# A hybrid SSD / chunk-MLP decoder step in float32: where activations are normalised, which engine does the element-wise work, and in which order the tiles of the input projection run

## The chip, the cores and the metric

The kernel runs on one core of a Trainium2 chip. A core has a matrix engine (TensorE, PE in the profile), three engines for element-wise work (VectorE or DVE, ScalarE or ACT, GpSimd or POOL), and a queue (SyncE, SP) that here only issues transfers. The metric is the device time of one execution in microseconds (us). The profile is one execution, recorded instruction by instruction.

## The reference, cut to what matters

288 tokens go through one layer: 256 of a prompt and 8 samples of 4 tokens each. The model dimension is 2048, and everything is float32.

```python
n = rmsnorm(h, g_mix)                       # x * rsqrt(mean(x*x) + eps) * g
proj = n @ w_in                             # 2048 -> 9248 columns, split into z, xbc, dt, u, v
xbc_c = silu(causal_dwconv(xbc, conv0))     # 4 taps along the tokens, 3072 channels
y, ssm_new = ssd(xs, dt, A, Bm, Cm, ssm0)   # four groups of eight heads, chunks of 128 tokens
y_ssd = grouped_rmsnorm((y + d_skip * xs) * silu(z))
u = gelu(u);  v = rmsnorm(gelu(v), g_cm)
y_cm = u * (tril(w_s) @ v + b_s)
h = h + concat([y_ssd, y_cm]) @ w_out
f = rmsnorm(h, g_ffn)
h = h + (silu(f @ w_gate) * (f @ w_up)) @ w_down
h = h + (p @ w_ple) * sigmoid(rmsnorm(h, g_pg) @ w_pg)
return rmsnorm(h, g_final), states
```

## The kernel before

**Layout and products.** Features lie on the 128 partitions and the 288 tokens along the free dimension. A weight tile is [128, 16, 128]: all 2048 inputs of 128 outputs. A float32 product is made of three: weights and activations are each split into two float32r parts, `hi` and `lo`, and `mm3` (L168) adds hi·hi, hi·lo and lo·hi in PSUM. In the trace these are the PE lines L171, L172 and L173, always 128x128 weights times 288 columns. `mtile` (L175) makes one output tile: it loads the weights (`load`, L154, 2048 columns or 1 MB in one transfer on SP's queue, three buffers), splits them 1024 columns at a time (`split_w`, L159: an ACT copy that rounds, L164, then a DVE subtraction, L165; three buffers each), and runs 48 products. 208 such tiles and 32 tiles of the down projection, with 22 input parts each, make nearly all of the PE's work.

**Start.** Fourteen products of ones warm the PE (L221). Then x (L227) and the first weights (L233) come in five parts that grow (`QUANTA`), and each part of x is split with the gain alone (L249). The two first output tiles and the 32 dt columns (L257, four row groups of PSUM at a time) are multiplied part by part. The root mean square of x is found beside it (`x_sumsq`, L261, on POOL and DVE); the projection is linear, so the factor of each token, `rs`, is multiplied into every projected tile later, by a DVE operation on its way out of PSUM (L347, L348, L539, L561).

**Input projection.** 24 tiles of x, B and C come first, each followed by `conv_tile` (L341): DVE applies `rs`, then the four taps run on 256 prompt columns and 32 sample columns apart (L357, L359), with POOL for the edges and the states. When a group's six tiles are there, `ssd_group` (L365) is appended to `side`, a list of Python generators; `advance` (L648) runs the next of them up to its `yield` after each tile, which puts the SSD's small matmuls between the long products. Then come the 16 tiles of the gate z (`z_tile`, L537), two tiles of v, the first half of the output projection (16 tiles), the rest of v, u with the spatial mix, the second half of the output projection, and the FFN.

**POOL's part before.** It forms Rh (L382), x times the decay (L406), the decay of the sample states h0 (L440), the gate product (L543), sums of squares (L134), the spatial mix of the samples (L627, L628) and others, and issues the smaller transfers.

**Order.** The instruction order within an engine comes from a planner in the tile framework, which simulates the program and takes what is ready, earlier lines of the program first. Each engine then runs its instructions in that order and waits on semaphores for the others.

**End.** After the last tile (gate of the input embedding) the final norm's sums (L101), the inverse square root (`rsqrt_compact`, L73, DVE, a chain of small operations), the broadcast (L111, L113) and the scaled output (L841, L843) follow one another.

Of the kernel before, what the change touches and what calls it, by code (L numbers as in the profile page):

```python
# [37 lines left out]
def hybrid_step(ctx: ExitStack, tc: tile.TileContext, xT, wa, wd, wple, pT, vec, cst, wdt, dtal,  # L38
# [51 lines left out]
    def rep4(pool, ap, eng=None):  # L90
        """[128, 32] -> [128, 128]: the sample tokens, four times over."""
        r = pool.tile([P, P], F32, tag="rep4", name="rep4", bufs=2 if pool is cp else 5)
        (eng or nc.gpsimd).tensor_copy(r3(r, 32), bc_mid(ap, 4))
        return r

    def sum_compact(acc):
        """Sums over the partitions of a [128, 288] tile, token-major."""
        ps = big()
        for c in range(3):
            lhs = acc[:, c * P:(c + 1) * P] if c < 2 else rep4(cp, acc[:, 256:288], nc.vector)  # L100
            nc.tensor.matmul(ps[:, c:c + 1], lhsT=lhs, rhs=ones[:, 0:1], start=True, stop=True)  # L101
# [5 lines left out]
    def bcast_tokens(r, keep_psum=False):  # L107
        """[128 tokens, 3] -> a slab with the value of each token on every partition."""
        ps = big()
        for c in range(2):  # L110
# [2 lines left out]
        nc.tensor.matmul(ps[:, 256:288], lhsT=r[0:32, 2:3].to_broadcast([32, P]),  # L113
                         rhs=ident[0:32, 0:32], start=True, stop=True)
# [44 lines left out]
    def split_w(raw, k0, n):  # L159
# [4 lines left out]
        nc.scalar.copy(a, r)  # L164
        nc.vector.tensor_sub(b, r, f32(a))  # L165
# [9 lines left out]
    def mtile(srcs, acts, loaded=None, ps=None):  # L175
        """One output tile: srcs are (dram view [128, k, 128]) in K order."""
        ps = pa.tile([P, NT], F32, tag="acc", name="acc") if ps is None else ps
        total, at = len(acts), 0
        for src in srcs:
            k = src.shape[1]  # L180
            raw = loaded.pop(0) if loaded else load(src, k)
            for k0 in range(0, k, 8) if k > 11 else ((0, 6) if k > 8 else (0,)):
# [758 lines left out]
```

## Time and profile before

| | us |
|---|---|
| median of 3 runs (1781.98 to 1783.4) | 1783.04 |
| span of the profiled execution | 1783.3 |
| busy: PE / weight loads | 1751.2 / 1715.2 |
| busy: DVE / ACT / POOL | 1106.4 / 752.8 / 401.7 |

The profiled execution's span is within 0.3 us of the median. "Busy" counts an engine's instructions from start to end; matmuls overlap, so PE's busy time says that something was in it, not that it ran at its peak. A matmul of two float32 operands appears as two PE records. "PEclk" and "clock" are the share of its full clock that the PE was granted.

### The profile page before, as it was taken

Reading aid. Unit: us, or ns where it says so; the run is one execution under the profiler, and the core shown is the slowest. Engines: PE = TensorE matmul, PEld = TensorE weight load, DVE = VectorE, ACT = ScalarE, POOL = GpSimd, SP = SyncE. Lnnn points to the kernel's source line nnn. Section 1 sums busy time; section 2 is a strip of 40 time slices with the busy share of each in tenths; the row PEclk is TensorE's granted clock in tenths of the full one; section 3 lists DMA queues with packets and bytes.
Section 4 is the critical chain, followed back from the end, with each engine's and each line's share of the span. In section 5 each row is a group of like instructions: output and inputs, shape, how many; then the busy total and the mean of one; then the engine's idle time right before and its main releaser. Section 6 shows DMA issues by size and latency. Waiting matters only on the chain.

```text
span 1783.3 us, 31260 instructions
## 1 busy us (share of the span) xinstructions
PE 1751.2 (98%) x12994; PEld 1715.2 (96%) x12994; DVE 1106.4 (62%) x1598; ACT 752.8 (42%) x1110; POOL 401.7 (23%) x500
## 2 busy tenths in 40 slices
PE   8989999999999999999999999999999999999996
PEld 7968988999999999999999999999999999999996
DVE  7989997865455676665555554444555555555654
ACT  4545544443345444443333333333333333454442
POOL 2665676420024531110000000000000000000133
PEclk9979999999999999999999999999999999999998
DMA  6525554744444444444444444555444444554542
GB/s 244 190 76 197 189 196 156 275 159 166 166 165 166 148 142 166 166 166 163 164 163 165 163 164 137 167 168 188 163 164 164 166 166 151 169 172 154 188 166 77
DMA packets 47084, 297.57 MB, mean 167 GB/s; under 512 B 5360, under 2 KB 6000, under 8 KB 18016
## 3 DMA queue, kind: packets, MB, share of 16 engines
q1 hardware_dynamic: 42544, 271.08, 44.7%
q0 software_dynamic: 3824, 23.34, 3.5%
q8 instruction: 101, 1.65, 0.4%
q10 hardware_dynamic: 576, 1.18, 0.2%
q14 instruction: 39, 0.32, 0.0%
HBM read 283.19 MB, written 12.39 MB: 166 GB/s over the span
## 4 chain that ended last, share of the span: by engine, by line
PE 93%; DVE 3%; issue 2%; POOL 1%; ACT 0%; DMA 0%; SPq 0%; DVEq 0%; POOLq 0%; ACTq 0%
PE acc L171 29%; PE acc L172 29%; PE acc L173 29%; DVE M L396 1%; DVE wlo L165 1%; PE pb L433 1%; PE pb L414 0%; POOL tm L627 0%; DMA xin<-in_xT_dram 0%; PE pb L171 0%; PE pb L173 0%; PE pb L172 0%; POOL sS L628 0%; PE pb L610 0%; PE pb L523 0%
## 5 line engine op out<-in xcount | busy, mean ns | idle before, releaser
L171 PE MATMUL acc<-hi,whi 128*128 128x288 f32 x3984 | 1183.3, 297 | 0.0
L172 PE MATMUL acc<-lo,whi 128*128 128x288 f32 x3984 | 1179.2, 296 | 0.0
L173 PE MATMUL acc<-hi,wlo 128*128 128x288 f32 x3984 | 1174.4, 295 | 0.0
L165 DVE TENSOR_TENSOR wlo<-raw,whi 128x1024 fp32r<-128x1024 f32 (+3 forms) x548 | 661.9, 1208 | 439.7 <-ACT whi L164 437.1
L164 ACT CAST whi<-raw 128x1024 fp32r<-128x1024 f32 (+3 forms) x548 | 539.1, 984 | 805.8 <-PE acc L172 757.4
L171 PEld LDWEIGHTS acc<-hi,whi 128*128 128x128 f32 x3984 | 749.6, 188 | 5.0 <-issue 4.3
L172 PEld LDWEIGHTS acc<-lo,whi 128*128 128x128 f32 x3984 | 750.8, 188 | 2.7 <-issue 1.8
L173 PEld LDWEIGHTS acc<-hi,wlo 128*128 128x128 f32 x3984 | 752.1, 189 | 1.3 <-issue 0.9
L798 POOL TENSOR_TENSOR Up<-Up,G 128x288 f32<-128x288 f32 x44 | 35.6, 810 | 666.9 <-DVE Up L797 652.7
L134 POOL TENSOR_TENSOR sacc<-sacc,sq 128x288 f32<-128x288 f32 x30 | 27.8, 926 | 226.4 <-ACT sq L133 226.4
L792 DVE TENSOR_TENSOR G<-acc,rs 128x288 f32<-128x288 f32 x44 | 20.1, 457 | 43.8 <-PE acc L173 43.8
L797 DVE SCALAR_TENSOR_TENSOR Up<-acc,rs 128x288 f32<-128x288 f32 x44 | 20.1, 457 | 42.6 <-PE acc L173 42.6
L357 DVE SCALAR_TENSOR_TENSOR cva<-cbuf,cwh,cva 128x256 f32<-128x256 f32 x72 | 43.9, 612 | 0.1
L576 POOL TENSOR_SCALAR vS<-ge,vec 128x32 f32<-128x32 f32 x16 | 6.9, 432 | 152.3 <-DVE ge L565 148.3
L440 POOL TENSOR_TENSOR h<-h,decS 128x512 f32<-128x512 f32 x32 | 37.4, 1199 | 0.1
L564 ACT ACTIVATE gt<-gt 128x288 f32<-128x288 f32 x32 | 14.2, 445 | 48.3 <-DVE gt L563 48.3
L144 DVE SCALAR_TENSOR_TENSOR lo<-h,vec,hi 128x288 fp32r<-128x288 f32 x32 | 33.7, 1053 | 0.0
L359 DVE SCALAR_TENSOR_TENSOR cva<-cbuf,cwh,cva 128x32 f32<-128x32 f32 x72 | 29.6, 411 | 2.8 <-POOL cva L355 2.4
L134 POOL TENSOR_TENSOR sacc<-sacc,G 128x288 f32<-128x288 f32 x14 | 18.8, 1341 | 48.8 <-ACT G L133 48.8
L360 ACT ACTIVATE cvt<-cva 128x288 f32<-128x288 f32 x24 | 10.6, 442 | 44.9 <-DVE cva L359 41.3
L642 POOL TENSOR_TENSOR u<-u,s 128x288 f32<-128x288 f32 x16 | 14.9, 939 | 63.9 <-DVE u L565 63.0
L149 ACT CAST hi<-Up 128x288 fp32r<-128x288 f32 x44 | 19.1, 434 | 21.5 <-POOL Up L798 21.5
(288 smaller groups left out, 1169.0 us busy)
## 6 DMA issues: line engine op xcount, KB each, us to landing
raw<-in_wa_dram SPq DMA_DIRECT2D x206, 1024.0 KB, 4.9
raw<-in_wd_dram SPq DMA_DIRECT2D x64, 704.0 KB, 4.1
h<-in_h0T_dram POOLq DMA_DIRECT2D x8, 1024.0 KB, 7.2
out_dram<-h POOLq DMA_DIRECT2D x8, 1024.0 KB, 4.9
h<-in_xT_dram POOLq DMA_DIRECT2D x4, 576.0 KB, 7.7
raw<-in_wple_dram SPq DMA_DIRECT2D x2, 1024.0 KB, 5.1
xin<-in_xT_dram SPq DMA_DIRECT2D x3, 576.0 KB, 8.4
out_dram<-h ACTq DMA_DIRECT2D x4, 288.0 KB, 3.0
```

The source lines that it names most:

```text
L134: nc.gpsimd.tensor_add(self.acc, self.acc, s)
L144: nc.vector.scalar_tensor_tensor(lo, x, gain, f32(hi), op0=ALU.mult, op1=ALU.subtract)
L164: nc.scalar.copy(a, r)
L165: nc.vector.tensor_sub(b, r, f32(a))
L171: nc.tensor.matmul(ps, lhsT=wh, rhs=hi, start=first, stop=False)
L172: nc.tensor.matmul(ps, lhsT=wh, rhs=lo, start=False, stop=False)
L173: nc.tensor.matmul(ps, lhsT=wl, rhs=hi, start=False, stop=last)
L357: nc.vector.scalar_tensor_tensor(a[:, 0:256], pr[:, j:j + 256], wt[j], a[:, 0:256], op0=ALU.mult, op1=ALU.add)
L359: nc.vector.scalar_tensor_tensor(asm, sa[:, :, j:j + 4], wt[j], asm, op0=ALU.mult, op1=ALU.add)
L440: nc.gpsimd.tensor_mul(r3(hh, 64), r3(hh, 64), bc_in(decS[:, 4 * q + i, hs], 64))
L792: nc.vector.tensor_mul(G, pg, rs)
L798: nc.gpsimd.tensor_mul(u, u, G)
```

## The change

The activations are normalised once, before the first product. All of x is loaded in eight parts, on SP's and ACT's queues; ACT squares each part, and 48 one-column matmuls add the squares of all 16 feature tiles in PSUM. From this come the inverse root, its broadcast to all partitions, and eight DVE multiplications of x; only then are the activations split. Three output tiles run side by side from there, and one dt matmul follows each feature tile. No projected tile is multiplied by `rs` any more.

POOL's tensor operations go to DVE and ACT, but for two multiplications at the very end; POOL keeps some memsets and the issue of transfers. The convolution runs on one row of 312 columns, prompt and samples together, and ACT copies the tile out of PSUM. Weights are loaded 1024 columns (512 KB) at a time with four buffers, and their split has a higher priority with the planner. From the second group on, z tiles of the group before are put between the convolution tiles, and gate and norm become generators of their own. The h0 states are handled in four parts instead of two, the v tiles run until the list of generators is empty, and the numbers of some buffers change (rs 1, slab 38, Rh 1, bm 2).

```diff
-    def rep4(pool, ap, eng=None):
-        (eng or nc.gpsimd).tensor_copy(r3(r, 32), bc_mid(ap, 4))
+    def rep4(pool, ap):
+        nc.scalar.copy(r3(r, 32), bc_mid(ap, 4))
+    def sum_tokens(ps, acc, first=True, last=True):
+        for c, t in enumerate((0, P, NT - P)):
+            nc.tensor.matmul(ps[:, c:c + 1], lhsT=acc[:, t:t + P], rhs=ones[:, 0:1], start=first and c == 0,
+                             stop=last and c == 2)
...
-            nc.gpsimd.tensor_add(self.acc, self.acc, s)
+            nc.vector.tensor_add(self.acc, self.acc, s)
...
     def load(src, k):
-        raw = st.tile([P, 2048], F32, tag="raw", name="raw")
+        raw = st.tile([P, 1024], F32, tag="raw", name="raw", bufs=4)
...
+        with tc.high_priority(offset=AHEAD):
+            nc.scalar.copy(a, r)
+            nc.vector.tensor_sub(b, r, f32(a))
...
+    def mtile(src, acts):
+        for k0 in range(0, total, 8):
+            n = min(8, total - k0)
+            w = split_w(load(src[:, k0:k0 + n], n), n)
+            for i in range(n):
+                mm3(ps, w, i, acts[k0 + i], k0 + i == 0, k0 + i == total - 1)
...
+    for q in range(8):
+        (nc.scalar if q % 2 else nc.sync).dma_start(xin[q], xT[:, 2 * q:2 * q + 2])
+    first = {(m, 0): load(wa[m, :, 0:8], 8) for m in range(3)}
+    pss = big("pss")
+    for q in range(8):
+        sq = s0.tile([P, 2, NT], F32, tag="sq", name="sq", bufs=4)
+        nc.scalar.activation(sq, xin[q], AF.Square)
+        for j in range(2):
+            sum_tokens(pss, sq[:, j], first=q + j == 0, last=q + j == 8)
+    halves = {at: split_w(raw, 8) for at, raw in first.items()}
+    rs0 = bcast_tokens(rsqrt_compact(pss[:, 0:3], 2048.0, EPS, "rm"), keep_psum=True)
+    for q in range(8):
+        nc.vector.tensor_mul(xin[q], xin[q], bc_mid(rs0, 2))
+        for k in (2 * q, 2 * q + 1):
+            xk = xin[q][:, k % 2]
+            n_act.append(split(xk, gain=vcol(V_MIX, k), tags=LONG))
+            for m in range(3):
+                if (m, k // 8) not in halves:
+                    halves[m, 1] = split_w(load(wa[m, :, 8:16], 8), 8)
+                mm3(ps01[m], halves[m, k // 8], k % 8, n_act[k], k == 0, k == KD - 1)
+            nc.tensor.matmul(pdt[32 * (k % 4):32 * (k % 4) + 32, 0:NT], lhsT=gw[:, k], rhs=xk,
+                             start=k < 4, stop=k >= 12, tile_position=(0, 32 * (k % 4)))
...
     def conv_tile(i, ps):
+        nc.scalar.copy(cb[:, 3:259], ps[:, 0:256])
+        nc.scalar.copy(new, r3(ps[:, 256:288], 4))
+        nc.scalar.activation(ao, cb[:, 0:NCO], AF.Identity, scale=wt[0], bias=cwh[:, i:i + 1])
         for j in range(1, 4):
+            nc.vector.scalar_tensor_tensor(ao, cb[:, j:j + NCO], wt[j], ao, op0=ALU.mult, op1=ALU.add)
+        nc.scalar.activation(to, ao, AF.Tanh)
...
-            nc.gpsimd.tensor_mul(r3(rh, P), bc_mid(T1, 4), bc_in(f32(dtAh[:, c, k:k + 4]), P))
+            for r, d in ((rh, dtAh), (rl, dtAl)):
+                for i in range(4):
+                    nc.scalar.activation(cols(r, i), T1, AF.Identity, scale=f32(d[:, c, k + i:k + i + 1]))
...
-            nc.gpsimd.tensor_mul(r3(xw, 64), r3(xd, 64), bc_in(dec[:, c, hs], 64))
+            for h in range(8):
+                nc.scalar.activation(xw[:, 64 * h:64 * h + 64], xd[:, 64 * h:64 * h + 64], AF.Identity,
+                                     scale=dec[:, c, 8 * g + h:8 * g + h + 1])
...
         def decay_h0(q):
-                nc.gpsimd.tensor_mul(r3(hh, 64), r3(hh, 64), bc_in(decS[:, 4 * q + i, hs], 64))
+                nc.vector.tensor_mul(r3(hh, 64), r3(hh, 64), bc_in(decS[:, 2 * q + i, hs], 64))
...
+    def z_tile(ps):
+        nc.scalar.activation(t, ps, AF.Tanh, scale=0.5)
+        nc.vector.scalar_tensor_tensor(zr, t, 1.0, ps, op0=ALU.add, op1=ALU.mult)
...
+    for g in range(4):
+        tiles = [16 + g, 20 + g] + list(range(4 * g, 4 * g + 4))
+        for j, i in enumerate(tiles):
+            ps = ps01[at] if at < 3 else mtile(wa[at], n_act)
+            if at == 0:
+                dt_work()
+                decay_work()
+                decay_sample()
+            at += 1
+            conv_tile(i, ps)
             advance(1)
+            if g and j in (1, 2, 4, 5):
+                zs.append(z_tile(mtile(wa[24 + 4 * (g - 1) + len(zs)], n_act)))
+                advance(1)
+        if g:
+            side.append(gate_group(g - 1, zs))
+        side.append(ssd_group(g))
+    for j in range(4):
+        zs.append(z_tile(mtile(wa[36 + j], n_act)))
+        advance(3)
```

More of the change, by code (lines that the diff above doesn't have):

```diff
@@ L173, in mm3 @@
         nc.tensor.matmul(ps, lhsT=wl, rhs=hi, start=False, stop=last)
[L175 to L182, printed above, removed]
-                n = min(8, k - k0) if k > 11 else ((6, k - 6)[k0 > 0] if k > 8 else k)
-                w = split_w(raw, k0, n)
-                for i in range(n):
-                    mm3(ps, w, i, acts[at], at == 0, at == total - 1)
-                    at += 1
+    def mtile(src, acts):
+        ps = pa.tile([P, NT], F32, tag="acc", name="acc")
+        total = len(acts)
+        for k0 in range(0, total, 8):
[3 more added lines that the diff above has]
+                mm3(ps, w, i, acts[k0 + i], k0 + i == 0, k0 + i == total - 1)
         return ps
@@ L211, in hybrid_step @@
     s0 = start.__enter__()
-    xin = [s0.tile([P, 4, NT], F32, name=f"xin{q}") for q in range(4)]
+    xin = [s0.tile([P, 2, NT], F32, name=f"xin{q}") for q in range(8)]
     wdts = s0.tile([P, KD, 32], F32, name="wdts")
@@ L238, in hybrid_step @@
-    w2 = load(wa[2], KD)
-    nc.sync.dma_start(csts, cst)
-    nc.sync.dma_start(dtals, dtal)
-    nc.sync.dma_start(scv, sconv)
-    xk = [xin[k // 4][:, k % 4] for k in range(KD)]
+    nc.scalar.dma_start(csts, cst)
+    first = {(m, 0): load(wa[m, :, 0:8], 8) for m in range(3)}
+    nc.scalar.dma_start(wdts, wdt)
+    nc.scalar.dma_start(dtals, dtal)
+    nc.scalar.dma_start(scv, sconv)
+    pss = big("pss")
[4 more added lines that the diff above has]
+            sum_tokens(pss, sq[:, j], first=q + j == 0, last=q + j == 8)
@@ L349, in conv_tile @@
-        nc.gpsimd.tensor_copy(cvo[:, i, 0], pr[:, 256:259])
-        nc.gpsimd.tensor_copy(cvo[:, i, 1:9], sa[:, :, 4:7])
-        a, t = slab(name="cva"), slab(name="cvt", tag="ta")
-        asm = r3(a[:, 256:288], 4)
+        sd = sd_box["pool"]
+        cb, a, t = (sd.tile([P, NCV], F32, tag=n, name=n, bufs=b) for n, b in (("cbuf", 3), ("cva", 2), ("cvt", 2)))
+        nc.gpsimd.memset(cb[:, 0:3], 0.0)
+        nc.scalar.copy(cb[:, 259:NCV].rearrange("p (b t) -> p b t", t=7)[:, :, 0:3], scv[:, i])
@@ L449, in ssd_group @@
         R0 = [make_R(0, hb) for hb in range(2)]
-        xrep = [rep4(sd, xs[j][:, 256:288]) for j in range(4)]
         yield
@@ L474, in ssd_group @@
         yield
+        xrep = [rep4(sd, xs[j][:, 256:288]) for j in range(4)]
         M1 = [seg(r) for r in R1]
@@ L512, in ssd_group @@
         nc.scalar.copy(xst, xwr)
-        for q in (32, 96):
-            nc.gpsimd.tensor_sub(xst[q:q + 32], xwr[q:q + 32], f32(xst[q:q + 32]))
-        decay_h0(0)
+        nc.vector.tensor_sub(xst[64:128], xwr[64:128], f32(xst[64:128]))
+        for q in range(4):
+            decay_h0(q)
         yield
@@ L684, in hybrid_step, with mlp_pools @@
-    nc.gpsimd.dma_start(o_conv, cvo)
-    pend = None
-    for g in range(4):
+    hp_box, mid_box = {}, []
+    def mlp_pools():
+        sd_pool.__exit__(None, None, None)
+        hp = ctx.enter_context(tc.tile_pool(name="hp", bufs=1))
+        h = hp.tile([P, KD, NT], F32, name="h")
+        mlp = tc.tile_pool(name="mlp", bufs=1)
+        mp = mlp.__enter__()
+        for q in range(4):
+            nc.gpsimd.dma_start(h[:, 4 * q:4 * q + 4], xT[:, 4 * q:4 * q + 4])
+        return hp, h, mlp, mp, spatial_weights(mp)
@@ L719, in hybrid_step @@
+    side.append(gate_group(3, zs))
+    nvt = 0
+    while side or nvt < 2:
+        v_tile(nvt, mtile(wa[56 + nvt], n_act), nv)
+        nvt += 1
+        advance(1)
+        if 3 in ssd_done and not hp_box and not any(x.__name__ == "ssd_group" for x in side):
+            hp_box["pools"] = mlp_pools()
+    hp, h, mlp_pool, mp, sw = hp_box["pools"]
     for m in range(KD):
-        ps = mtile([wa[40 + m]], ycat[:16])
+        ps = mtile(wa[40 + m], ycat[:16])
         nc.vector.tensor_add(h[:, m], h[:, m], ps)
-    for i in range(2, KD):
-        ps = mtile([wa[56 + i]], n_act)
+    for i in range(nvt, KD):
+        ps = mtile(wa[56 + i], n_act)
```

263 lines of the change are left out of this document (86 added, 177 removed).

## The prediction

> **What bounds the kernel now.** The page comes first: span, busy times, clock line, chain by engine.
>
> ```profile
> span 1783.3 us, 31260 instructions
> PE 1751.2 (98%) x12994; PEld 1715.2 (96%) x12994; DVE 1106.4 (62%) x1598; ACT 752.8 (42%) x1110; POOL 401.7 (23%) x500
> PEclk9979999999999999999999999999999999999998
> PE 93%; DVE 3%; issue 2%; POOL 1%; ACT 0%; DMA 0%; SPq 0%; DVEq 0%; POOLq 0%; ACTq 0%
> ```
>
> PE holds 93% of the chain. Faster element-wise work is worth something only where PE waits or runs at a lower clock. The view of stretches says where that is (stretch, length, busy of PE with records, of PEld, DVE, ACT, POOL, granted clock, DMA):
>
> ```profile
> 0.00:40.00 40.00, 31.41 (x205) 27.55 (x206) 31.90 (x41) 17.59 (x30) 13.01 (x14) 0.91 0.69 246
> 80.00:112.00 32.00, 32.00 (x205) 27.35 (x207) 29.02 (x56) 19.61 (x48) 22.59 (x33) 0.89 0.31 107
> 112.00:140.00 28.00, 20.96 (x139) 17.87 (x132) 22.37 (x26) 4.70 (x6) 14.48 (x19) 0.76 0.12 39
> 140.00:200.00 60.00, 59.15 (x408) 50.84 (x408) 58.67 (x104) 29.50 (x61) 41.05 (x64) 0.97 0.55 198
> 200.00:300.00 100.00, 100.00 (x725) 86.86 (x723) 87.38 (x144) 49.97 (x101) 70.64 (x84) 1.00 0.52 188
> 300.00:350.00 50.00, 49.46 (x358) 48.15 (x358) 42.36 (x74) 21.96 (x36) 23.95 (x25) 0.97 0.72 265
> 600.00:650.00 50.00, 49.12 (x381) 48.72 (x380) 36.77 (x64) 21.71 (x34) 26.98 (x40) 1.00 0.42 136
> 650.00:1764.00 1114.00, 1114.00 (x8377) 1113.68 (x8377) 609.14 (x759) 456.70 (x613) 107.82 (x118) 1.00 0.48 162
> ...
> 87.20:94.10 6.90, 6.90 (x29) 6.34 (x30) 6.35 (x13) 3.19 (x11) 4.73 (x8) 0.52 0.44 153
> 118.00:131.60 13.60, 8.74 (x40) 7.57 (x41) 11.16 (x12) 1.49 (x2) 7.80 (x10) 0.51 0.08 11
> ```
>
> From 650 to 1764 us PE never stops: 1114.00 / 8377 = 0.133 us a record. Nothing that the change does to the FFN can show there. A stretch's loss is its idle time plus half of the busy time that it spent at half clock (clock 0.89 over 32 us means 7 us at half):
> - 112 to 140: 7.0 idle, and half of the 8.7 busy us of 118 to 131.6, together 11.4 us
> - 80 to 112: 3.5; 140 to 200: 0.85 + 1.8 = 2.7; 300 to 350: 0.5 + 1.5 = 2.0; 600 to 650: 0.9
> - 0 to 40: 8.6 idle, of which 1.5 lies before the first product, and 3.4 for the clock, so 10.5 after it.
>
> About 31 us in all, 20 of them after the start. That, and the time to the first product, is what can change.
>
> **The part that it removes.** The timeline explains 112 to 140:
>
> ```profile
> 100.89 0.68 DVE L396 TENSOR_TENSOR M<-M,cbm 128x512 f32<-128x512 f32 x1
> ...
> 112.85 9.95 DVE L396 TENSOR_TENSOR M<-M,cbm 128x512 f32<-128x512 f32 x1
> ...
> 113.54 8.03 POOL L440 TENSOR_TENSOR h<-h,decS 128x512 f32<-128x512 f32 x8
> ```
>
> The same DVE mask takes 0.68 us and, where eight POOL decays run back to back, 9.95. PE waits for it and then runs at half clock. With these products off POOL, the 11.4 us go. The spatial mix leaves POOL too (0.9). Of the other 8.2 us (3.5 + 2.7 + 2.0) most is clock, after spells of narrow matmuls (below), which stay in the program; I count 2 as gained by the z tiles between them, between 0 and 8.2. The stage takes on work for which I put 2 us of new stalls (0 to 20, third rival). Stage: -11.4 - 0.9 - 2 + 2 = -12.3 us.
>
> **The part that it adds: the start.** Products now wait for all of x, 48 one-column sums, a root and a broadcast. The old start:
>
> ```profile
> 0.99 5.32 PE L221 MATMUL warm<-ones 128*128 128x128 f32 x28 [0.99 <-POOL cbuf L345]
> 6.78 0.40 PE L171 MATMUL ps<-hi,whi 128*128 128x288 f32 x1 [0.46 <-ACT whi L164]
> ...
> L101 PE MATMUL pb<-ones,sacc 128*128 128x1 f32 x32 | 4.0, 229 | 0.0
> L257 PE MATMUL pdt<-xin,gw 128*32 128x288 f32 x32 | 3.5, 466 | 0.0
> L488 PE MATMUL pb<-S,cva 128*128 128x512 f32 x8 | 4.4, 632 | 0.0
> ```
>
> The first product runs at 6.8. In the new start the warm-up ends at 6.3 as before; x (2.4 MB) needs about 9 to 10 us at the 246 GB/s of the first 40 us, so the sums, not the loads, decide. L101 has two records a matmul (32 for 16), so 48 sums are 96 records. Their rate hangs on the clock:
>
> ```profile
> 1.20:5.20 4.00, 4.00 (x20) 4.00 (x21) 1.00 0.82 206
> 5.40:6.40 1.00, 0.91 (x9) 0.72 (x7) 1.00 0.87 293
> ...
> 85.80:87.20 1.40, 1.40 (x14) 0.93 0.00 0
> 87.20:88.00 0.80, 0.80 (x4) 0.50 0.00 0
> ...
> 0.00:10.00 10.00, 8.48 (x49) 7.21 (x49) 3.95 (x6) 4.43 (x8) 2.50 (x8) 1.00 0.81 258
> 10.00:20.00 10.00, 4.89 (x31) 3.29 (x31) 10.00 (x5) 8.35 (x15) 9.73 (x6) 0.83 1.04 403
> ```
>
> The first two rows are the warm-up alone (L221): 0.2 us a record until 5.2, then 0.11, so the clock doubles at about 5.3 (the clock column shows no lower clock there, but the spacing does). The next two are L332, matmuls of 32 columns: 0.1 us a record, then 0.2; the clock falls at 87.2 although PE had work all the time. Narrow matmuls do not hold the clock. The two low stretches shown above last 6.9 and 13.6 us, two and four times 3.4, so I take 3.4 us as the grain: the next decision after 5.3 falls at 8.7, in a stretch with 1 us of warm-up and otherwise one-column sums, and I expect half clock from there. Then 21 records at 0.112 us from 6.3 to 8.7 and 75 at 0.213 (the slow warm-up's spacing, nearer than any other row), 16.0 us: the last sum is at 24.7. At full clock all along it would be 6.3 + 96 x 0.112 = 17.1.
>
> On this point the Trainium skill ("TensorE: Matmul & The Clock Gate", Part 1) says that a monitor of how busy the PE is sets the clock, and that sustained activity of some 3.4 us releases it. Read plainly, a steady run of sums would keep the clock, and the sum would be that of the first rival; the L332 row, where it fell in the middle of such a run, is against it.
>
> From the sums to the first product, the tail of the old kernel has the same steps:
>
> ```profile
> 1768.99 0.36 PE L101 MATMUL pb<-ones,rep 128*128 128x1 f32 x2
> 1773.59 0.40 ACT L837 COPY rsb<-pb 128x288 f32<-128x288 f32 x1 [5.12 <-PE pb L113]
> ...
> L843 DVE TENSOR_TENSOR h<-h,pb 128x576 f32<-128x576 f32 x6 | 4.1, 748 | 2.3 <-ACT rsb L837 2.3
> ...
> L143 ACT ACTIVATE hi<-xin,vec 128x288 fp32r<-128x288 f32 x16 | 7.4, 525 | 5.1 <-DMA xin<-in_xT_dram 5.1
> ```
>
> 1769.3 (end of the sums) to 1773.6 is 4.2 us with the broadcast at half clock, 3.4 at full. One scaling of two feature tiles takes 0.75, one rounding 0.53. First product: 24.7 + 4.2 + 0.75 + 0.53 = 30.2 us (full clock: 21.7).
> The splits that feed PE then:
>
> ```profile
> L144 DVE SCALAR_TENSOR_TENSOR lo<-cva,vec,hi 128x288 fp32r<-128x288 f32 x16 | 8.2, 544 | 0.2 <-ACT hi L143 0.2
> ...
> L164 ACT CAST whi<-raw 128x1024 fp32r<-128x1024 f32 x418 | 437.8, 1048 | 637.8 <-PE acc L172 592.1 <-issue 30.3 <-PE ps L172 3.2
> ...
> 103.56 1.21 DVE L165 TENSOR_TENSOR wlo<-raw,whi 128x1024 fp32r<-128x1024 f32 x1
> ```
>
> For two feature tiles DVE needs 0.75 + 2 x 0.54 = 1.8 us, PE 18 products, 2.4, so PE sets the pace.
>
> Further terms:
> - The dt matmuls lose their neighbours in the other row groups. Before, 32 records took 3.5 us. Alone, a record scales from L488 (4.4 / 8 = 0.55 at 512 columns, 0.31 at 288, with overlap about 0.24): 7.7 to 9.9 us in place of 3.5. I take the lower, +4.3.
> - The old sums and the old broadcast of the root, 12 records of 0.12, leave this place: -1.5.
> - The old stalls of the start go: -10.5.
> - New stalls: three buffers each of whi and wlo hold the first halves of three tiles until their last product, so the second halves are split while PE waits: a copy of 1.05 and three subtractions of 1.2 against about 2 us of other work, 1.5 to 3; I take 1.5. And about 2 at half clock until it rises again (1 to 3.4).
>
> Start: (30.2 - 6.8) + 4.3 - 1.5 - 10.5 + 3.5 = +19.2 us. Written for the time T of the first product, start and stage together give 1783.3 + T - 23.3.
>
> **What I cost at nothing.**
>
> ```profile
> SPq L156 <- DVE wlo L165: 1510.3, 258, 24.5
> ```
>
> The missing `rs` product, DVE's sums of squares and gate products in the FFN: from 650 on DVE is busy for 609 of 1114 us, and PE waits for none of it; some 0.45 us more for each 12.8 us changes no product's start. Loads of 512 KB: SP's queue waits for free buffers (1510 us for L165, the row above), not for data, and four buffers hold 2 MB, or 12.8 us of products; uncovered, a late load would cost its lateness at each of some 440 places, which I find unlikely at a DMA share of 0.48. The tail keeps its chain; the column scaling that moves from POOL to ACT lies beside the sums.
>
> **The rivals.**
> - *The clock stays full during the sums.* T = 21.7 and 1.5 us of new stalls for 3.5: 1783.3 + 21.7 - 23.3 - 2.0 = 1779.7. For it: the clock stayed full in the first 10 us and fell to 0.83 only in the next ten, with few products. Against it: L332. It is the way that the Trainium skill's rule, above, would have it.
> - *The sums hide behind the loads* (faster). If weight loads for one-column products run well under 0.11 us, the sums end with x at about 11 us: T = 11 + 3.4 + 1.3 = 15.7, 1783.3 + 15.7 - 23.3 - 2.0 = 1773.7. It decides at T = 23.3, or 25.3 with those smaller stalls; from 21.7 down the kernel is faster by 0.2% or more. Against it: 4.0 us for 32 records of L101.
> - *ACT becomes the bound of the SSD stage.*
>
> ```profile
> L384 ACT ACTIVATE Rl<-cst,dtAl 128x128 fp32r<-128x128 f32 x64 | 20.4, 390 | 4.6 <-PE pb L390 4.6
> ...
> L466 ACT COPY btm<-pb 128x256 f32<-128x256 f32 x4 | 1.4, 360 | 2.5 <-PE pb L464 2.5
> ```
>
>   From 200 to 300 ACT is busy for 50 us and DVE for 87. A group gains on ACT 16 pieces of Rh, 24 of x times decay, the copies out of PSUM and the states of six tiles, at up to 0.36 to 0.39 us each in the rows above and about 0.2 for the smallest, some 20 us, and the z tiles' share of splits. I estimate 65 to 70 of 83 us (ten tiles of 6.4 and the SSD's own matmuls) for both engines, close enough that short pieces ahead of a weight copy could stop PE at each tile: 40 tiles x 0.3 = 12 us more, 1802.
> - *The planner orders it otherwise*, so that little of this happens: around 1783.
>
> **How the numbers follow.** Forecast 1783.3 + 19.2 - 12.3 = 1790.2, so 1790; span and median differ by 0.3 us, so no correction. Its own range is 1784 to 1797 (the dt term, the clock after the start, 0 to 8.2 of narrow spells). Chances: forecast 0.50, full clock 0.22, ACT 0.17, hidden sums 0.06, planner 0.05. 0.2% (3.6 us) is about what a measurement of this kernel can tell from no change. Faster: half of the full clock, the hidden sums, a part of the planner, 0.19. Same: the other half, the forecast's lower end, 0.22. Slower: 0.59. The range leaves out the hidden sums, the low end of full clock, and half of the ACT case: 1775 to 1803.
>
> **What would show it.** PE's L-line of the sums with 96 records and its spacing (0.11 or 0.21); the first product near 30; no DVE mask over 1 us; no stall between 112 and 140 but a low clock after the narrow spells; ACT's busy share of the SSD stage near 80%; 0.133 us a record in the FFN as before. A first product before 20, or a spacing in the FFN other than 0.133, would make the prediction wrong.

## The result and the profile after

The changed kernel takes 1803.66 us (median of 4 runs, 1801.47 to 1804.6) against 1783.22 for the kernel before: the ratio is 1.0102, with a 95% interval of 1.0084 to 1.012. (It is not the quotient of these two medians, 1.0115, which the interval holds too.) The changed kernel is 1.0% slower. The profiled execution of the changed kernel took 1801.47 us, its span is 1799.3; in all profiled runs below the device time is about 2 us above the span. Spans are compared with spans.

The page of the changed kernel, span, busy times and granted clock in 40 slices:

```profile
span 1799.3 us, 31672 instructions
...
PE 1765.1 (98%) x13084; PEld 1731.5 (96%) x13084; DVE 1062.1 (59%) x1655; ACT 826.9 (46%) x1432; POOL 31.2 (2%) x79
...
PEclk6999999999999999999999999999999999999998
```

POOL does next to nothing now (401.7 us before), ACT has gained 74 us, and PE is still busy for 98% of the span. Two slices of the clock have changed visibly: the first has fallen from 0.9 to 0.6, and the third has risen from 0.7 to 0.9. The view of stretches, whose columns are those of the prediction, has the rest:

```profile
10.90:31.50 20.60, 20.59 (x96) 20.55 (x96) 4.59 (x5) 7.53 (x12) 0.00 (x0) 0.50 0.54 189
...
80.00:112.00 32.00, 32.00 (x239) 31.53 (x239) 21.29 (x37) 24.42 (x69) 0.40 (x4) 1.00 0.44 147
112.00:140.00 28.00, 28.00 (x201) 21.95 (x200) 21.17 (x37) 19.73 (x57) 0.65 (x2) 1.00 0.35 123
140.00:200.00 60.00, 60.00 (x452) 59.17 (x452) 46.28 (x91) 35.06 (x84) 4.78 (x13) 1.00 0.63 213
200.00:300.00 100.00, 100.00 (x733) 91.80 (x732) 76.55 (x145) 73.38 (x198) 5.51 (x16) 1.00 0.52 170
300.00:350.00 50.00, 50.00 (x371) 44.20 (x371) 41.84 (x77) 27.53 (x70) 4.81 (x9) 1.00 0.61 193
350.00:420.00 70.00, 65.54 (x465) 58.03 (x464) 50.25 (x103) 42.28 (x106) 7.08 (x14) 0.95 0.47 157
420.00:445.00 25.00, 18.97 (x121) 17.93 (x121) 13.30 (x23) 7.50 (x11) 0.34 (x1) 0.86 0.72 264
...
900.00:1300.00 400.00, 400.00 (x3010) 400.00 (x3009) 204.20 (x247) 147.41 (x169) 0.00 (x0) 1.00 0.52 165
```

Three things are to be seen. From 80 to 350 PE is busy all the time at clock 1.00, where before it stood 7 us between 112 and 140 and ran at 0.76 to 0.97 in four of the stretches: by the prediction's rule (idle time plus half of the time at half clock) all of the 3.5 + 11.4 + 2.7 + 2.0 us are gone. In the first row 96 records take 20.6 us at clock 0.50: the sums. And two stretches in which the kernel before had no loss have one now: 350 to 420 (4.5 idle, clock 0.95) and 420 to 445 (6.0 idle, clock 0.86), together 10.5 us idle and up to 7 us for the clock, some 15 to 17. The last row is the FFN: 400 / 3010 = 0.133 us a record, as before. The kernel before in the two stretches:

```profile
350.00:420.00 70.00, 70.00 (x528) 69.68 (x527) 49.92 (x91) 34.60 (x52) 17.91 (x16) 1.00 0.47 163
420.00:445.00 25.00, 25.00 (x192) 25.00 (x191) 11.29 (x13) 8.42 (x8) 0.00 (x0) 1.00 0.50 169
```

**The start.** The timeline of the changed kernel (start, length, engine, line; in brackets the idle time before it and what ended it):

```profile
5.04 0.34 ACTq L229 DMA_DIRECT2D cst<-in_cst_dram  x1
6.64 0.34 ACTq L231 DMA_DIRECT2D wdts<-in_wdt_dram  x1
8.34 0.34 ACTq L232 DMA_DIRECT2D dtal<-in_dtal_dram  x1
9.79 0.33 ACTq L233 DMA_DIRECT2D scv<-in_sconv_dram  x1
10.17 2.40 ACT L239 ACTIVATE sq<-xin 128x576 f32<-128x576 f32 x4 [7.49 <-DMA cst<-in_cst_dram]
...
10.91 2.29 PE L102 MATMUL pss<-ones,sq 128*128 128x1 f32 x10 [3.69 <-ACT sq L239]
...
35.50 5.41 DVE L249 TENSOR_TENSOR xin<-xin,pb 128x576 f32<-128x576 f32 x8 [1.58 <-PE pb L120]
...
36.88 0.85 PE L179 MATMUL ps<-hi,whi 128*128 128x288 f32 x2 [1.42 <-ACT hi L150]
...
37.90 3.78 PE L257 MATMUL pdt<-xin,gw 128*32 128x288 f32 x32
```

The first product is at 36.9 us, not 6.8. ACT issues four small loads ahead of its first square, and they leave its queue only 1.5 to 1.7 us apart, though each takes 0.34. So the first square comes at 10.2, PE stands idle from the end of the warm-up to 10.9, and the 96 sums run at half clock from the first to the last. (The bracket of the square names the load of cst. That load landed 6.2 us after its issue, at 11.2, which is after the square had begun, so it is not what the square waited for.) Behind the sums and the root, DVE scales all eight parts of x, 5.41 us, before it computes its first lo. The dt products, in one block, fill PE's time until the first product with a lo runs at 41.6.

**The stall at 366 to 372.** The timeline there:

```profile
366.73 1.27 ACT L366 ACTIVATE Rl<-cst,dtAl 128x128 fp32r<-128x128 f32 x4
...
367.90 2.01 ACT L389 ACTIVATE xw<-xdt,dec 128x64 f32<-128x64 f32 x8
368.06 0.50 PE L372 MATMUL pb<-Rl,Ur 128*128 128x512 f32 x1 [1.60 <-ACT Rl L366]
369.81 0.53 ACT L150 ACTIVATE hi<-cvo,vec 128x288 fp32r<-128x288 f32 x1
...
370.37 0.52 DVE L151 SCALAR_TENSOR_TENSOR lo<-cvo,vec,hi 128x288 fp32r<-128x288 f32 x1 [2.43 <-ACT hi L150]
370.90 0.82 DVE L526 SCALAR_TENSOR_TENSOR zr<-zt,acc 128x288 f32<-128x288 f32 x2
...
371.41 0.61 PE L179 MATMUL acc<-hi,whi 128*128 128x288 f32 x1 [2.86 <-DVE zr L526]
```

Read from below: PE waits 2.86 us for an accumulator that zr, the DVE product that empties a z tile, has not emptied; zr stands on DVE behind a lo; lo waits 2.43 for its hi; and hi stands on ACT behind eight 64-column pieces of the weighted x (xw). The four pieces before those, Rl (the lo part that goes with Rh), made PE wait 1.60.

**The stall at 430 to 435**, in the timeline, and behind it three lines of the DMA view of 410 to 440 (transfers: number, KB each, us from issue to landing):

```profile
432.09 2.29 DVE L576 TENSOR_TENSOR wsr<-wsr,cst 128x2048 f32<-128x2048 f32 x1 [5.00 <-DMA wsr<-in_wsT_dram]
434.30 1.18 DVE L707 TENSOR_TENSOR h<-h,acc 128x288 f32<-128x288 f32 x3
...
434.89 0.58 PE L179 MATMUL acc<-hi,whi 128*128 128x288 f32 x1 [4.41 <-DVE h L707]
```

```profile
raw<-in_wa_dram SPq DMA_DIRECT2D x7, 512.0 KB, 5.9
h<-in_xT_dram POOLq DMA_DIRECT2D x4, 576.0 KB, 7.1
wsr<-in_wsT_dram POOLq DMA_DIRECT2D x1, 1024.0 KB, 12.6
```

The mask of the spatial weights (L576), on POOL before, is on DVE now. It waits 5.00 us there for a load that takes 12.6 us beside four parts of h and seven weight loads, and holds up three residual additions (L707) that would have emptied accumulators: PE waits 4.41.

### The profile page after: what moved, and what is told of

Same layout as the page of the kernel before. It is cut to its first block, busy times and chain, and to the rows that moved or that the text cites. A ratio compares the mean times of both kernels' runs of the same rounds, so it can differ in the third digit from the quotient of the medians.

```text
span 1799.3 us, 31672 instructions
## 1 busy us (share of the span) xinstructions
PE 1765.1 (98%) x13084; PEld 1731.5 (96%) x13084; DVE 1062.1 (59%) x1655; ACT 826.9 (46%) x1432; POOL 31.2 (2%) x79
## 4 chain that ended last, share of the span: by engine, by line
PE 75%; DVE 0%; ACT 0%; DVEq 0%; issue 0%
PE acc L179 25%; PE acc L181 24%; PE acc L180 24%; PE pb L597 0%; PE pb L181 0%; PE pb L179 0%; PE pb L180 0%; PE pb L589 0%; DVE h L829 0%; PE pb L102 0%; PE pb L118 0%; DVE wlo L173 0%; DVE h L707 0%; PE pb L120 0%; DVEq L916 0%
## 5 line engine op out<-in xcount | busy, mean ns | idle before, releaser
L172 ACT CAST whi<-raw 128x1024 fp32r<-128x1024 f32 (+1 forms) x516 | 533.7, 1035 | 827.8 <-PE acc L180 664.8
L173 DVE TENSOR_TENSOR wlo<-raw,whi 128x1024 fp32r<-128x1024 f32 (+1 forms) x516 | 623.3, 1208 | 486.2 <-ACT whi L172 479.5
L778 DVE TENSOR_TENSOR G<-acc,rs 128x288 f32<-128x288 f32 x44 | 20.1, 457 | 41.6 <-PE acc L181 41.6
L338 DVE SCALAR_TENSOR_TENSOR cva<-cbuf,cwh,cva 128x312 f32<-128x312 f32 x72 | 38.5, 538 | 1.3 <-ACT cva L336 0.4
L389 ACT ACTIVATE xw<-xdt,dec 128x64 f32<-128x64 f32 x96 | 24.4, 338 | 5.9 <-DVE xdt L386 5.9
L102 PEld LDWEIGHTS pss<-ones,sq 128*128 128x128 f32 x96 | 20.6, 333 | 3.9 <-ACT sq L239 3.9
L102 PE MATMUL pss<-ones,sq 128*128 128x1 f32 x96 | 20.6, 352 | 3.7 <-ACT sq L239 3.7
L418 DVE TENSOR_TENSOR h<-h,pb 128x512 f32<-128x512 f32 x32 | 20.9, 680 | 1.1 <-PE pb L417 1.1
L366 ACT ACTIVATE Rh<-cst,dtAh 128x128 fp32r<-128x128 f32 x64 | 20.6, 397 | 1.5 <-PE pb L371 1.5
L784 DVE TENSOR_TENSOR Up<-Up,G 128x288 f32<-128x288 f32 x44 | 20.2, 458 | 1.5
L366 ACT ACTIVATE Rl<-cst,dtAl 128x128 fp32r<-128x128 f32 x64 | 20.8, 399 | 0.0
```

The costliest lines, as they stand in the source:

```text
L102: nc.tensor.matmul(ps[:, c:c + 1], lhsT=acc[:, t:t + P], rhs=ones[:, 0:1], start=first and c == 0, stop=last and c == 2)
L338: nc.vector.scalar_tensor_tensor(ao, cb[:, j:j + NCO], wt[j], ao, op0=ALU.mult, op1=ALU.add)
L366: nc.scalar.activation(cols(r, i), T1, AF.Identity, scale=f32(d[:, c, k + i:k + i + 1]))
L389: nc.scalar.activation(xw[:, 64 * h:64 * h + 64], xd[:, 64 * h:64 * h + 64], AF.Identity, scale=dec[:, c, 8 * g + h:8 * g + h + 1])
L418: nc.vector.tensor_add(h0[q][:, i], h0[q][:, i], ps)
L784: nc.vector.tensor_mul(u, u, G)
```

## The experiments

The theory: the change gains about 20 us in the SSD stage by taking work off POOL; it loses 30 at the start; and it adds two waits in queues that had room before. The main rival for each part was that the loss has another cause and only moves. Eleven kernels were run. "T" is the first product, "rest" the span less T: what a start costs shows in T, what a later stall costs in the rest. Each ratio is against the kernel before as it ran beside that experiment (medians of 1782.49 to 1784.55). Span, T and rest are of one profiled execution each; the spans of one kernel differ by 1 to 5 us between its executions, so a difference of less than 2 or 3 us in the rest counts only where the medians agree.

| kernel | median us | ratio (95%) | span | T | rest |
|---|---|---|---|---|---|
| before | 1783.22 | | 1783.3 | 6.78 | 1776.5 |
| changed | 1803.66 | 1.0102 (1.0084, 1.012) | 1799.3 | 36.88 | 1762.4 |
| e1 mask on POOL | 1797.64 | 1.0083 (1.0068, 1.0098) | 1796.8 | 36.59 | 1760.2 |
| e2 wide sums | 1794.85 | 1.0065 (1.005, 1.008) | 1794.3 | 29.75 | 1764.6 |
| e3 small loads off ACT | 1794.96 | 1.0066 (1.0051, 1.0081) | 1793.3 | 30.00 | 1763.3 |
| e4 before, decay on DVE | 1769.07 | 0.9929 (0.9911, 0.9948) | 1766.3 | 6.31 | 1760.0 |
| e5 mask moved | 1801.53 | 1.0103 (1.0084, 1.0122) | 1801.6 | 36.94 | 1764.7 |
| e6 z first | 1802.9 | 1.011 (1.0091, 1.0128) | 1801.4 | 36.95 | 1764.5 |
| e7 before, start free of POOL | 1763.19 | 0.9888 (0.9867, 0.9908) | 1760.0 | 6.78 | 1753.2 |
| e8 all parts | 1790.07 | 1.0038 (1.0024, 1.0052) | 1788.6 | 24.55 | 1764.1 |
| e9 mask after the root | 1796.23 | 1.0069 (1.005, 1.0088) | 1793.0 | 36.71 | 1756.3 |
| e10 weighted x on DVE | 1794.09 | 1.0056 (1.004, 1.0072) | 1795.1 | 36.69 | 1758.4 |
| e11 four mends | 1779.38 | 0.9968 (0.9958, 0.9979) | 1776.6 | 24.06 | 1752.5 |

### The start: e2 and e3

e2 makes the sums 128 columns wide instead of one:

```diff
-            sum_tokens(pss, sq[:, j], first=q + j == 0, last=q + j == 8)
+            for c, t in enumerate((0, P, NT - P)):
+                nc.tensor.matmul(pss[:, c * P:(c + 1) * P], lhsT=sq[:, j, t:t + P], rhs=ones,
+                                 start=q + j + c == 0, stop=q + j == 8 and c == 2)
```

> The changed kernel with the 48 sums of the start 128 columns wide instead of one (the ones matrix whole as moving operand, the root read from one column of each block); the same number of records and weight loads. My theory: the 0.213 us a record of the sums is the half clock, and it is half because one-column products do not count as work for the clock. Expected: the clock stays or becomes full during the sums, 0.112 us a record, the sums take 11 to 14 us instead of 20.6, first product 7 to 10 us earlier, span 1789 to 1793. Rival: the sums are bound by loading 128x128 float32 weights at the start, whatever the clock counts; then wide sums take as long or longer (0.213 or more a record) and the span does not fall.

The view of stretches of e2, cut where the granted clock changes:

```profile
9.60:16.40 6.80, 5.44 (x26) 5.44 (x27) 1.68 (x3) 4.21 (x7) 0.00 (x0) 0.51 1.02 380
16.40:26.70 10.30, 8.03 (x72) 7.84 (x71) 4.76 (x15) 3.94 (x6) 0.00 (x0) 0.99 0.57 180
```

The same 96 records begin at the same time, at 0.21 us each (5.44 / 26), but the clock then rises and the others take 0.112 (8.03 / 72). T falls by 7.1 us. With one column the clock stayed at 0.50 for 20.6 us although PE was busy for 20.59 of them. The Trainium skill ("TensorE: Matmul & The Clock Gate", Part 1) has the clock released by some 3.4 us of sustained activity. These two runs show that the one-column matmuls did not count as such activity and the 128-column ones did.

e3 issues the small loads from POOL:

```diff
-    nc.scalar.dma_start(csts, cst)
+    nc.gpsimd.dma_start(csts, cst)
...
-    nc.scalar.dma_start(scv, sconv)
+    nc.gpsimd.dma_start(scv, sconv)
```

> The changed kernel with four small loads of the start (constants, dt weights, dt vectors, convolution states) issued by POOL instead of ACT. My theory: ACT stands in these issues until 10.1 us because its queue takes no more than the four parts of x at once, so the first square starts at 10.2 although x's first part landed some 4 us earlier. Expected: first square at 5 to 6 us, first sum right after the warm-up at 7 to 7.5, sums end 3 to 4 us earlier, and since little idle time is left between warm-up and sums the clock may stay full for one more stretch of 3.4 us: span 3 to 6 us shorter, 1793 to 1796. Rival: the squares wait for x to land, not for the issues; then nothing moves by more than 1 us.

The timeline of e3:

```profile
6.26 18.42 PE L102 MATMUL pss<-ones,sq 128*128 128x1 f32 x96
...
30.00 0.85 PE L179 MATMUL ps<-hi,whi 128*128 128x288 f32 x2 [1.41 <-ACT hi L150]
```

The sums begin at 6.26, right behind the warm-up, and end at 24.7. The four loads alone cost 6.9 us. What holds ACT's queue is not shown directly: in the changed kernel SP's queue, too, issued nothing between its four parts of x and 5.2 us, and there the view of waits names the loads of x as what it waited for. In all of after, e2, e3 and e8 the rest of the kernel is the same within 2.2 us (1762.4 to 1764.6): each microsecond of T is a microsecond of the time.

### The stage before: e4 and e7

e4 is the kernel before with one word changed, the decay of h0 on DVE:

```diff
-                nc.gpsimd.tensor_mul(r3(hh, 64), r3(hh, 64), bc_in(decS[:, 4 * q + i, hs], 64))
+                nc.vector.tensor_mul(r3(hh, 64), r3(hh, 64), bc_in(decS[:, 4 * q + i, hs], 64))
```

> The kernel before with one part of the change alone: the decay of the sample states (32 products of 128x512) on DVE instead of POOL. My theory: the stall of the kernel before at 112 to 140 us is one DVE mask held up for 9.9 us beside eight of these products on POOL. Expected: no DVE mask over 1.5 us, no stall there, span 8 to 12 us shorter than 1783.3, 1771 to 1775, although DVE gets 22 us more work. Rival: DVE is already busy for 80 to 97% in this stage, so 22 us more on it delay the weight splits, and the span stays or grows (1783 to 1795).

The view of stretches of e4:

```profile
80.00:112.00 32.00, 32.00 (x216) 26.01 (x214) 29.74 (x56) 20.02 (x49) 23.08 (x34) 0.95 0.32 108
112.00:140.00 28.00, 27.65 (x207) 25.52 (x204) 28.00 (x54) 12.79 (x26) 17.68 (x21) 1.00 0.39 127
140.00:200.00 60.00, 59.40 (x435) 52.54 (x434) 59.74 (x117) 31.49 (x64) 30.59 (x58) 1.00 0.62 212
```

PE's records from 112 to 140 go from 139 to 207 at clock 1.00, and the kernel is 0.7% faster. Its span is 17.0 us shorter, more than the 8 to 12 expected, since the losses after 140 have shrunk as well: in the third row above, 2.7 us have become 0.6 of idle time, and from 300 to 350 2.0 have become 0.2 (0.24 idle, clock 1.00). In e4 no z tiles stand between the convolution tiles. So most of what the kernel before lost there went with the decays, and z tiles were not needed for it. The loss before 112 cannot be the decays', whose first runs at 113.5; it is 3.5 us in the kernel before, 1.6 in e4 and 0.4 in e7 below, with the same sixteen 32-column matmuls (L332) in each, and what decides it stays open.

The Trainium skill ("SBUF — State Buffer", Who interferes with whom) says that a DVE instruction with two inputs in SBUF and a GpSimd instruction that reads SBUF exclude each other. The runs agree that one waits for the other. The DVE mask of 9.95 us shows more than that: DVE can be kept out over all of eight POOL instructions in a row, not over one.

The largest loss left in e4 is of the same kind (timeline of e4):

```profile
10.29 2.59 POOL L264 TENSOR_TENSOR sq<-xin 128x1152 f32<-128x1152 f32 x1 [0.72 <-DMA xin<-in_xT_dram]
...
10.84 9.73 DVE L144 SCALAR_TENSOR_TENSOR lo<-xin,vec,hi 128x288 fp32r<-128x288 f32 x4
...
12.96 2.74 POOL L266 TENSOR_TENSOR sq<-sq,sq 128x1152 f32<-128x1152 f32 x1
...
15.66 4.60 POOL L264 TENSOR_TENSOR sq<-xin 128x1152 f32<-128x1152 f32 x2
...
21.77 0.61 PE L173 MATMUL ps<-hi,wlo 128*128 128x288 f32 x1 [7.23 <-DVE wlo L165]
```

Four lo that take 1.80 us elsewhere take 9.73 beside POOL's squares and the addition between them, which run without a pause worth naming from 10.3 to 20.3. e7 takes them off POOL too:

```diff
-            nc.gpsimd.tensor_mul(sq[q], xin[q], xin[q])
+            nc.scalar.activation(sq[q], xin[q], AF.Square)
...
-                nc.gpsimd.tensor_add(sq[0], sq[0], sq[1])
+                nc.vector.tensor_add(sq[0], sq[0], sq[1])
```

> The kernel before with the decay on DVE, as in e4, and also the start's squares on ACT and their first add on DVE, so that POOL has no tensor work while the first products run. Theory (the largest loss left in e4, 7.5 us at 14 us, was a lo of DVE held up beside POOL's squares): it goes, and 1769 becomes 1757 to 1764. Rival (ACT's squares of 0.9 to 1.1 us each stand between the early copies and the first products wait for those instead): 1766 to 1772, no gain over e4.

1763.19 us: within the theory, and the fastest kernel of all, 1.1% below the one before, with three lines changed. The stretch from 0 to 42 of e7, where PE was busy for 33.41 us at clock 0.92 in the kernel before:

```profile
0.00:42.00 42.00, 37.81 (x270) 34.07 (x271) 29.39 (x59) 25.00 (x39) 3.64 (x14) 1.00 0.76 268
```

### The mask of the spatial weights: e1, e5, e9

e1 puts L576 back on POOL:

```diff
-        nc.vector.tensor_mul(w, w, bc_mid(T1, KD))
+        nc.gpsimd.tensor_mul(w, w, bc_mid(T1, KD))
```

> The changed kernel with one instruction put back: the mask of the spatial weights (128x2048) runs on POOL, not DVE. My theory: in the changed kernel DVE stands for 5.0 us before this mask, which waits for its weights from HBM, and 2.3 us in it, with three residual additions and three weight splits queued behind; PE idles for 6.5 us between 420 and 437 us and then has half clock for 6.8. Expected: DVE takes the additions before 432, PE does not stop there, span 8 to 9 us shorter than the changed kernel's 1799.3, about 1791. Rival: the additions wait for h itself, which is loaded just before (10 us to landing); then the stall stays, only the 2.3 us of the mask go, and the span is 1797.

It gained less than the theory asked for. The profiled execution has a span of 1796.8, the rival's number, but it is the longest of its four, and that of the changed kernel is the shortest of its four; the medians are 6.0 us apart. The rival's reason is not what happened: the additions begin at 431.1 and have waited for PE, not for h. A line of the timeline of e1, the instructions of the tile wlo in e1, between 432 and 443 (minimum, median and maximum in ns), and PE's stretch:

```profile
431.14 1.18 DVE L707 TENSOR_TENSOR h<-h,acc 128x288 f32<-128x288 f32 x3 [2.90 <-PE acc L181]
```

```profile
L173 DVE TENSOR_TENSOR wlo<-raw,whi x4: 1212/1214/5618, 432.2 to 440.0; 128x1024 fp32r<-128x1024 f32 x4
```

```profile
420.00:445.00 25.00, 20.70 (x149) 19.53 (x148) 17.89 (x29) 8.21 (x11) 7.13 (x5) 1.00 0.80 293
```

The wait for the load went to POOL, where nothing waits behind it; but then the mask runs 5.48 us on POOL, from 432.4, and one weight subtraction on DVE takes 5.6 us instead of 1.2. It is the kind of collision that e4 removed, at another place. PE still idles for 4.3 us, but its clock stays at 1.00.

e5 moves the product in the program, to the first line of `spatial`, and keeps it on DVE:

```diff
-        nc.vector.tensor_mul(w, w, bc_mid(T1, KD))
         return bss, wss, w, b
...
     def spatial(nv, mp, bss, wss, w, b):
+        nc.vector.tensor_mul(w, w, bc_mid(T1, KD))
```

> The changed kernel with one DVE instruction moved: the product of the spatial weights with the mask is issued at the start of the spatial step and no longer where the weights' loads are issued; it stays on DVE. Theory (DVE stood 5 us before this product, for a load that had not landed, with the residual adds and a lo of the product stream queued behind it, and PE lost 8 to 9 us at 420 to 440 with the half clock that followed): the stall there goes, 1801.5 becomes about 1793, and DVE has no wait of over 1 us for a DMA at that line. Rival (the loads saturate the DMA share there and PE waits for weights anyway): within 3 us of the changed kernel, the wait only moves to another line.

Nothing happened: the timeline of e5 has the product, from its new line, in the same place and with the same wait.

```profile
434.02 2.29 DVE L579 TENSOR_TENSOR wsr<-wsr,cst 128x2048 f32<-128x2048 f32 x1 [4.78 <-DMA wsr<-in_wsT_dram]
436.23 1.18 DVE L707 TENSOR_TENSOR h<-h,acc 128x288 f32<-128x288 f32 x3
```

The planner makes the order, and it takes what is ready by its own simulation, in which the load is presumably there by then (not shown). So e5 says nothing about the cause. e9 gives the product a third factor, a one computed from the root of v, so that it has to come later:

```diff
-        nc.vector.tensor_mul(w, w, bc_mid(T1, KD))
...
+        one = mp.tile([P, 1], F32, name="one")
+        nc.vector.tensor_scalar(one, r[:, 0:1], 0.0, 1.0, op0=ALU.mult, op1=ALU.add)
+        nc.vector.scalar_tensor_tensor(w, w, one[:, 0:1], bc_mid(T1, KD), op0=ALU.mult, op1=ALU.mult)
```

> e5 changed nothing, since the order of DVE's work is made by the planner and it put the moved product back in front of the residual adds. Here the same product on DVE has a third factor, a one worked out from the root of v, so that it can only come after the v tiles. Theory (DVE's 5 us wait for a load in front of the residual adds is the cause of the stall at 420 to 437 us): with it gone PE loses less than 2 us there, and 1801.5 becomes 1792 to 1795. Rival (the residual itself, or the weights, land as late, since the DMA share is 1.0 there): the wait moves to the residual adds or a weight copy and the time stays within 3 us.

```profile
420.00:445.00 25.00, 22.51 (x164) 21.58 (x164) 14.07 (x21) 10.30 (x13) 0.00 (x0) 1.00 0.82 291
```

This stretch of e9 has 164 records where the changed kernel has 121, and the clock stays at 1.00. The rest falls by 6.1 us (1762.4 to 1756.3), the median by 7.4, to just above the 1792 to 1795 expected. The theory holds, with 2.5 us of idle time still there, short waits for split weights.

### The z tiles: e6 and e10

e6 puts the Tanh and zr of a z tile at the planner's high priority:

```diff
-        nc.scalar.activation(t, ps, AF.Tanh, scale=0.5)
-        nc.vector.scalar_tensor_tensor(zr, t, 1.0, ps, op0=ALU.add, op1=ALU.mult)
+        with tc.high_priority(offset=AHEAD):
+            nc.scalar.activation(t, ps, AF.Tanh, scale=0.5)
+            nc.vector.scalar_tensor_tensor(zr, t, 1.0, ps, op0=ALU.add, op1=ALU.mult)
```

> The changed kernel with the two operations that empty a z tile's accumulator (ACT's Tanh and DVE's product) at the high priority that the product stream's splits have. Theory (PE waited 3 us at 368 us for an accumulator that zr had not yet emptied, since zr stood on DVE behind a lo that waited for ACT's small pieces, and half clock followed, 7 us in all): PE's wait there falls below 1 us and 1801.5 becomes 1795 to 1798. Rival (ACT is simply full there and the order of its queue is what counts): zr comes no earlier, since its Tanh stands behind the same pieces, and the time stays within 2 us.

DVE took some zr earlier than before, but the time did not change, as the rival had it. The waits of e6 between 360 and 380 (us in total, times, longest) are those of the changed kernel:

```profile
PE acc L179 <- DVE zr L527: 2.9, 1, 2.9
...
DVE lo L151 <- ACT hi L150: 2.6, 2, 2.4
```

e10 instead shortens what stands ahead on ACT:

```diff
-            for h in range(8):
-                nc.scalar.activation(xw[:, 64 * h:64 * h + 64], xd[:, 64 * h:64 * h + 64], AF.Identity,
-                                     scale=dec[:, c, 8 * g + h:8 * g + h + 1])
+            nc.vector.tensor_mul(r3(xw, 64), r3(xd, 64), bc_in(dec[:, c, hs], 64))
```

> The changed kernel with the weighted x of the SSD stage as one DVE product of 128x512 in place of eight ACT pieces of 128x64. Theory (the stall at 366 to 376 us comes from ACT's queue: Rl and hi stand behind eight pieces of 2.0 us in all, lo waits for hi, and zr and the accumulator for lo): PE's waits there shrink from 4.5 us to below 1, the half clock behind them goes, and 1801.5 becomes 1794 to 1796. Rival (the group is full anyway: DVE gains 24 x 0.7 = 17 us in all, its lo come later and PE waits for those): 1799 to 1806.

Waits and the stretch from 360 to 380 in e10:

```profile
PE acc L179 <- DVE zr L524: 0.9, 1, 0.9
```

```profile
360.00:380.00 20.00, 19.13 (x132) 15.66 (x131) 17.13 (x30) 13.67 (x34) 0.55 (x1) 1.00 0.41 132
```

The wait is 0.9 us, the clock 1.00, the rest 4.0 us shorter; the median is 9.6 lower, and the profiled execution, at 1796.88 us, is the longest of its four. The cause of this stall is ACT's row of small pieces.

### Together: e8 and e11

e8 joins e2, e3, e5 and e6 and writes all dt products behind the product stream's, with the first splits at high priority.

> The changed kernel with the parts together: sums 128 columns wide, the small loads issued by POOL, the mask product later, the z tiles' two operations first, and at the start all dt products behind the product stream's, with the splits of the first tiles at high priority. Theory (each part was its own loss): the gains of the wide sums (6.6) and of the small loads (6.5) overlap in part, about 10 together; the mask 8, z 4 to 6, the dt products 2 to 4: 1772 to 1780, below the kernel before. Rival (the losses stand in one chain, and taking one away uncovers the next): 1785 to 1792, no better than the kernel before.

It came to 1790.07, on its rival's side. T fell by 12.3 us, and that is all: the rest is no shorter (1764.1). Its parts for the mask and the z tiles did nothing, as e5 and e6 show, and the planner kept the order at the start: eight scalings before the first lo, and the dt products in one block meanwhile. The four parts of e11 are those of e2, e3, e9 and e10:

> The changed kernel with wide sums, the small loads issued by POOL, the mask product after the root (e9) and the weighted x on DVE (e10). The first two together brought the first product to 24.8 us and 11.5 us in e8. Theory (three separate losses, so the gains add up): 1790 less what e9 and e10 gain, 1774 to 1780 if both theories hold, faster than the kernel before by 0.2 to 0.5%. Rival (one or both stalls have another cause): 1783 to 1790.

1779.38 us, 0.3% faster than the kernel before, within the theory. T is 12.8 lower than in the changed kernel, and the rest 9.9, where e9 (6.1) and e10 (4.0) alone give 10.1. By these single executions the losses are separate and add up. By the medians they do so only in the main: e9 is 7.4 and e10 9.6 below the changed kernel, with the 12.8 of the start 29.8, and e11 is 24.3 below it. PE still idles for 3.8 us from 350 to 420 in e11, in short waits of which the largest, 2.0 in all, are for the subtractions of weights.

## Why the prediction was right or wrong

The direction was right, and so were the two sides of the sum: a start that waits for the sums at half clock, against a gain in the SSD stage. The size was not: 1790 forecast, 1803.7 measured, 0.7 above the range (by the ratio, 1.0102 times the 1783.04 that the forecast set out from, 1801.2, just inside it). These are the terms, one by one.

- **The first product** (30.2 predicted, 36.9 measured) is the step that failed most: the term "the sums begin at the end of the warm-up". The working looked at when x lands and at PE, not at ACT's queue, where four more loads are issued ahead of the first square. Every instruction of the moved step was to be counted, and these were left out. The sums begin at 10.9 instead of 6.3: the warm-up took 0.9 us longer, at half clock throughout (6.22 us for its 28 records, 0.22 each), and PE then stood for 3.7. With the four loads on POOL (e3) the rest of that working holds almost to the digit: last sum 24.7 (predicted 24.7), first product 30.0 (30.2).
- **The clock in the sums** was right. The rival of the full clock is refuted: 0.213 us a record was predicted, 20.6 / 96 = 0.215 measured. e2 shows it from the other side. In e3 the clock is 1.00 until 8.7 us and 0.53 from 8.7 to 9.1, the time that the working gave; there is some luck in that, since the warm-up of e3 (5.43 us) had its full clock about when that of the kernel before had it (5.32), and that of the changed kernel did not.
- **Root, broadcast, scaling, rounding**: 4.2 + 1.3 predicted; 4.0 from the last sum (31.5) to the first scaling (35.5), and 1.4 to the first product.
- **After the first product** -4.2 us was predicted (+4.3 for dt, -1.5, -10.5, +3.5). By difference, in the profiled executions, it came out 4 to 6 us better, and the dt term is 4.0 of that: +4.3 for 32 products alone (its own figures, 7.7 less 3.5, give 4.2), but they take 3.78 us against 3.5 before. That PE sets the pace from the first product on was wrong, too: DVE scaled all eight parts before its first lo, and the dt products ran while PE would have waited for it.
- **The gain of the stage** was too small: of the 8.2 us of narrow spells I counted 2 as gained, by the z tiles, and all are gone; the collision's 11.4 went as predicted. With the spatial mix that is 20.5 us in place of 14.3. The reason given was wrong in part: of the 4.7 us after 140 the decays' move alone takes all but 0.8 (e4; 1.7 in e7), with no z tile between. What removes the 3.5 before 112 is not shown.
- **The new stalls** were put at 2 us in the stage (0 to 20); they cost 15 to 17. The third rival named the engine of the first (366 to 372), ACT's short pieces, but as 0.3 us at each of 40 tiles, not as one wait of 4.5 us with its half clock. ACT's 73.4 of 100 us from 200 to 300 is less than the 65 to 70 of 83 that I had estimated (78 to 84%), and no tile there waits. The second, a 5 us wait for a load on DVE, I had not seen: I costed the mask as removed work of POOL and not as a waiting instruction added to DVE.
- **At nothing**: the FFN's rate is what it was, 0.133 us a record, and no loss was found for the loads of 512 KB there. Right.
- **The planner** did order some of it otherwise, the fourth rival, though not to 1783: the dt products in one block ahead of the stream, and each edit that only moved a line or raised a priority (e5, e6, the dt part of e8) left its wait in place.

In spans: start +30.1, rest -14.1, together +16.0 (1783.3 to 1799.3). The prediction had +23.4 and -16.5, so by the spans the start carries most of the error, 6.7 of 9.1 us, and in the rest two errors nearly cancel, which is luck: new stalls not foreseen, and old ones gone that I had left standing. The medians differ by 4.4 us more than the spans do: by the 2 us between span and time the profiled execution of before lies about 2 us above its median, while that of the changed kernel is its shortest, 2.2 below. Where these 4.4 us lie is not known; if they are in the rest, its error is as large as that of the start.

## What to carry to other kernels

Taking work off an engine moves its waits too: an instruction that waits for a load holds up all that stands behind it on its new engine, so it must not be put ahead of instructions that empty accumulators. Before a step is moved to the front, list every instruction of its engine's queue there, transfers among them, and ask whether the matmuls it needs are wide enough to hold the clock. And if one collision is what the profile shows, remove it by itself first: three lines gave 1.1% here, where the rebuilt kernel lost 1.0%.

## What was not expected of the hardware

- One-column matmuls back to back for 20.6 us, PE busy throughout, never raised the clock from 0.50; the same sums 128 columns wide raised it after about 5.4 us of work. Sixteen matmuls of 32 columns (L332) were followed by half clock in the kernel before (0.52 from 87.2 to 94.1) and not in e7 (1.00 from 80 to 112), so one short narrow run does not settle the clock.
- A DVE operation with two inputs in SBUF beside POOL work can last until POOL's run of instructions is over: 9.95 us beside eight (0.68 alone), 5.6 us beside one of 5.48 (1.2 alone). Not every one does: at 96.5 us of the kernel before the same mask took 0.69 while POOL was at work on the weighted x, whose instruction took 1.57 there and 1.03 at 111.8.
- Transfers issued by ACT behind four loads of x left its queue 1.5 to 1.7 us apart, though each took 0.34. Whether the number of transfers under way limits it was not tried.
